# mLSTM gate projection, row-maximum broadcast and denominators in other forms, and the SBUF pools in another order

## The chip, the cores and the metric

One NeuronCore of one Trainium2 chip runs the whole program in one launch. The metric is device time in microseconds of that core, the median of several runs. The kernel before takes 2479.89 us (three runs, 2475.71 to 2484.41). TensorE is the matrix engine, VectorE (DVE), ScalarE (ACT) and GpSimd (POOL) work on tiles of 128 partitions, and SyncE (SP) issues the loads.

## What is computed

Two transformer blocks follow each other on 256 tokens of width 2048, all in float32. The first is attention and a gated feed-forward layer. The second, where the change stands, is an mLSTM beside a gated convolution. Cut to what matters:

```python
proj = h @ w_in[l] + b_in[l]
(q, k, v, o, z_a, i_pre, f_pre, u, b_gate, c_gate, z_b, g_a, g_b) = jnp.split(proj, split_points, axis=-1)
...
b = jnp.cumsum(lf, axis=-1)                       # lf = log_sigmoid(f_pre)
d_intra = b[..., :, None] - b[..., None, :] + li[..., None, :]
m_row = jnp.maximum(d_inter, jnp.max(d_intra, axis=-1))
scores = jnp.einsum('bhld,bhsd->bhls', qb, kb) * jnp.exp(d_intra - m_row[..., None])
num = jnp.einsum('bhls,bhsv->bhlv', scores, vb) + ...
den = jnp.sum(scores, axis=-1) + ...
h_out = num / jnp.maximum(jnp.abs(den), jnp.exp(-m_row))[..., None]
```

There are 8 heads with keys of 128 and values of 256. `i_pre` and `f_pre` are 8 columns each: the projection of the gates is 2048 to 16, beside others of 2048 to 2048.

## The kernel before, in words

A large product is made in fp32r, a fast form of float32, three times over: each operand is split into a high part (`hi`, `khi`) and the rest (`lo`, `klo`), and hi*hi, lo*hi and hi*lo are added in PSUM (`group_mm`, L321 to L323). The work is a list of steps. A step loads a block of weights of 128x2048 (1 MB) into one of four tiles `raw`, splits it (ScalarE makes `hi`, L245, VectorE `lo`, L246) and does 24 matmuls of 512 columns. Loads and splits run ahead of the matmuls by the number of buffers. `later(n, f)` puts a small piece of work behind the matmuls of the step n further on. A scheduler orders the instructions of each engine from this program, by priorities and its own estimate of times; each engine then runs its list in that order.

The second block starts behind a barrier (`barrier2`: norm of the residual, transposes, splits). Then come the steps for v (4 groups of 4 steps), the gates (one step), and four times q/k, o and z_a, with two heads behind each z_a. The rest of the block (`ga`, `u`, `cg`, `bg`, `zb`, `gb`, projections) has no part in the change.

- The gates (`if_step`): weights padded to 128 columns, loaded and split as any step; 3 x 16 x 2 matmuls with 128 moving columns (L983 to L985). `if_rows` turns the result, on 8 partitions, into cumulated rows, their running maximum M and four small transposes (`rowT`).
- A head (`mlstm`) has four pieces. `s1` makes the scores, and a copy of row h of M on all 128 partitions (`mb`, L1082: weights are one column of the identity, repeated, over the 8 partitions of M, in plain float32). `s2` sums the weighted scores over the keys: against a column of ones for the denominators (`den`, L1100 to L1102, three float32 products with one moving column), against the values for the numerators (`num`, L1103 to L1105, three of 256 columns). Six loads of the same three weight tiles belong to them.
- `row_bcast` (L350) copies a gain over all partitions, with a 128x128 tile of ones as weights.
- `pe_gemv` (L194), an adaptive row, is not changed. It is 16 float32 products with 128 moving columns, whose outputs lie on four strips of 32 partitions in turn. The prediction uses its times.

The tiles live in pools which lie one behind the other in SBUF in the order in which the program opens them: single tiles (`persist`), `kp` (40 tiles of 2048 bytes a partition), `zp`, `tp`, `wp` (raw), `hp` (hi, lo), `sp` (small).

## Time and profile before

| what | before |
|---|---|
| median of three runs | 2479.89 us (2475.71 to 2484.41) |
| the profiled execution | 2476.79 us, span 2475.0 us, granted TensorE clock 0.991 |
| TensorE busy | 2410.0 us (97%), 12508 matmul records |
| VectorE busy | 1584.8 us (64%) |
| ScalarE busy | 1151.2 us (47%) |
| DMA | 597.36 MB, 241 GB/s |

The span is the time from the first to the last instruction in the profile; the execution around it is 1.8 us longer. Busy shares are means over the span. A matmul row of the trace gives start, life and count; a float32 product stands there as two records. The granted clock is TensorE's: 1.00 is 2.4 GHz, 0.50 is 1.2 GHz.

### The profile page before, as it was taken

To read this page: it belongs to the slowest core of one execution; us is meant where nothing else is said; L and a number is where in the kernel's file an instruction comes from. 1 tells how busy PE (TensorE), PEld (TensorE's weight loads), DVE (VectorE), ACT (ScalarE), POOL (GpSimd) and SP (SyncE) were. 2 spreads that over 40 slices of the span, in tenths; PEclk is the share of its full clock that TensorE was granted. 3 is DMA by queue.
4 is the path that set the end of the run, shared out by engine and by line. 5 is a ranking of instruction groups with operands and counts; after the bars stand their busy time and mean duration, and the time that the engine had idled before them with its cause. 6 is when DMAs were issued, how large, how long until landed. Compare 5 with 4: busy or idle time off the path is not lost.

```text
span 2475.0 us, 30384 instructions
## 1 busy us (share of the span) xinstructions
PE 2410.0 (97%) x12508; PEld 2023.7 (82%) x12508; DVE 1584.8 (64%) x1727; ACT 1151.2 (47%) x1415; POOL 0.2 (0%) x4
## 2 busy tenths in 40 slices
PE   6999989999999999999899999999999999999998
PEld 4888988878888888888778888888888888888887
DVE  5888888876666566666664556565456666554555
ACT  5433887653443433334553335455333443444344
POOL 0000000000000000000000000000000000000000
PEclk9999999999999999999999999999999999999999
DMA  8987879847777677677635554555557667555553
GB/s 319 339 332 276 312 280 356 335 187 278 287 266 283 252 282 290 240 298 285 217 115 205 184 191 177 188 178 191 187 211 250 242 249 251 201 198 209 189 193 132
DMA packets 90436, 597.36 MB, mean 241 GB/s; under 512 B 10165, under 2 KB 10805, under 8 KB 20665
## 3 DMA queue, kind: packets, MB, share of 16 engines
q1 hardware_dynamic: 90296, 595.41, 66.1%
q8 instruction: 98, 1.61, 0.3%
q14 instruction: 42, 0.34, 0.0%
HBM read 593.28 MB, written 2.10 MB: 241 GB/s over the span
## 4 chain that ended last, share of the span: by engine, by line
PE 89%; DVE 4%; ACT 3%; DMA 3%; issue 1%; SPq 0%; ACTq 0%; DVEq 0%
PE gu L322 6%; PE gu L321 6%; PE gu L323 6%; PE dn L322 3%; PE dn L323 3%; PE dn L321 3%; PE wo L322 2%; PE wo L321 2%; PE wo L323 2%; PE v L321 2%; PE v L322 2%; PE v L323 2%; DVE lo L246 2%; DMA graw<-i_ada_k 2%; PE z_a L321 1%; PE ga L321 1%
## 5 line engine op out<-in xcount | busy, mean ns | idle before, releaser
L246 DVE TENSOR_TENSOR lo<-raw,hi 128x2048 fp32r<-128x2048 f32 (+3 forms) x446 | 917.1, 2061 | 715.2 <-ACT hi L245 714.9
L245 ACT ACTIVATE hi<-raw 128x2048 fp32r<-128x2048 f32 (+3 forms) x446 | 769.1, 1730 | 1037.2 <-PE gu L323 251.3
L321 PE MATMUL gu<-hi,khi 128*128 128x512 f32 x688 | 268.3, 390 | 0.0
L322 PE MATMUL gu<-lo,khi 128*128 128x512 f32 x688 | 267.8, 389 | 0.0
L323 PE MATMUL gu<-hi,klo 128*128 128x512 f32 x688 | 267.7, 389 | 0.0
L172 DVE SCALAR_TENSOR_TENSOR graw<-graw,cb 128x2048 f32<-128x2048 f32 x112 | 255.9, 2285 | 11.1 <-DMA graw<-i_w_ada 8.7
L322 PEld LDWEIGHTS gu<-lo,khi 128*128 128x128 f32 x688 | 129.2, 188 | 26.8 <-DVE lo L246 0.2
L323 PEld LDWEIGHTS gu<-hi,klo 128*128 128x128 f32 x688 | 129.2, 188 | 26.7
L321 PEld LDWEIGHTS gu<-hi,khi 128*128 128x128 f32 x688 | 129.1, 188 | 26.5
L322 PE MATMUL dn<-lo,khi 128*128 128x512 f32 x336 | 131.0, 390 | 1.5 <-DVE lo L246 1.5
L323 PE MATMUL dn<-hi,klo 128*128 128x512 f32 x336 | 130.8, 389 | 0.0
L321 PE MATMUL dn<-hi,khi 128*128 128x512 f32 x336 | 130.5, 390 | 0.0
L285 PE MATMUL qk<-h,lo 128*128 128x256 f32 x256 | 74.7, 292 | 3.1 <-DVE lo L246 3.1
L283 PE MATMUL qk<-h,hi 128*128 128x256 f32 x256 | 75.7, 296 | 0.1
L322 PEld LDWEIGHTS dn<-lo,khi 128*128 128x128 f32 x336 | 63.1, 188 | 15.2 <-DVE lo L246 2.4
L284 PE MATMUL qk<-h,hi 128*128 128x256 f32 x256 | 74.3, 290 | 0.0
L509 PE MATMUL e<-h,lo 128*128 128x256 f32 x256 | 72.8, 287 | 1.6 <-DVE lo L246 1.6
L323 PEld LDWEIGHTS dn<-hi,klo 128*128 128x128 f32 x336 | 63.1, 188 | 13.2
L321 PEld LDWEIGHTS dn<-hi,khi 128*128 128x128 f32 x336 | 63.1, 188 | 13.1
L507 PE MATMUL e<-h,hi 128*128 128x256 f32 x256 | 73.7, 289 | 0.0
L508 PE MATMUL e<-h,hi 128*128 128x256 f32 x256 | 72.9, 286 | 0.0
L285 PEld LDWEIGHTS qk<-h,lo 128*128 128x128 f32 x256 | 51.0, 199 | 3.5 <-DVE lo L246 3.5
(439 smaller groups left out, 4987.1 us busy)
## 6 DMA issues: line engine op xcount, KB each, us to landing
raw<-i_w_gu SPq DMA_DIRECT2D x88, 1024.0 KB, 4.8
graw<-i_ada_t SPq DMA_DIRECT2D x64, 1024.0 KB, 5.9
graw<-i_w_ada SPq DMA_DIRECT2D x48, 1024.0 KB, 4.8
raw<-i_w_dn SPq DMA_DIRECT2D x44, 1024.0 KB, 4.8
graw<-i_ada_k SPq DMA_DIRECT2D x32, 1024.0 KB, 7.0
raw<-i_w_out SPq DMA_DIRECT2D x32, 1024.0 KB, 5.7
raw<-i_w_s SPq DMA_DIRECT2D x24, 1024.0 KB, 6.8
raw<-i_w_qk SPq DMA_DIRECT2D x16, 1024.0 KB, 7.3
```

The lines of the kernel that those rows point to most:

```text
L172: dve.scalar_tensor_tensor(g, g, 1.0, cb, op0=OP.mult, op1=OP.mult, accum_out=dst)
L245: act.activation(hi[:, b:e], r[:, b:e], AF.Copy)
L246: dve.tensor_sub(lo[:, b:e], r[:, b:e], hi[:, b:e].bitcast(F32))
L283: pe.matmul(dst, wh, K[k][:, 0, :], start=s, stop=False)
L284: pe.matmul(dst, wh, K[k][:, 1, :], start=False, stop=False)
L285: pe.matmul(dst, wl, K[k][:, 0, :], start=False, stop=e)
L321: pe.matmul(dsts[th], xh, wh, start=s, stop=False)
L322: pe.matmul(dsts[th], xh, wl, start=False, stop=False)
L323: pe.matmul(dsts[th], xl, wh, start=False, stop=e)
L507: pe.matmul(dst, hv[:, i, c0:c0 + 128], H[k][:, 0, :], start=(k == k0), stop=False)
L508: pe.matmul(dst, hv[:, i, c0:c0 + 128], H[k][:, 1, :], start=False, stop=False)
L509: pe.matmul(dst, lv[:, i, c0:c0 + 128], H[k][:, 0, :], start=False, stop=(k == k1 - 1))
```

## The change

Five edits go together.

- The gates' weights are loaded as they are (128x256, 128 KB), without a step of their own: loaded behind the third group of v, multiplied behind the fourth. The products are plain float32 with 16 weight columns; the inputs are the hi and the lo part one after the other. Block k writes to the strip of partitions 32 (k mod 4); ScalarE copies the four strips into a zeroed tile `ifp`, and two steps later one float32 product with a 0/1 matrix (`mlc["sel"]`) adds them up (`ifq`).
- M is split into hi and lo on partitions 0 to 7 and 32 to 39 of a 64-partition tile (`mhl`), and `mb` is one fp32r product with a repeated column of a 0/1 matrix (`msel`).
- A value tile gets a column of ones behind each 256 values (2 x 260 columns, 2080 bytes), and the denominators come out as column 256 of `num`. There are two output tiles, and ScalarE reads the two columns singly.
- `row_bcast` takes one column of ones, repeated, as weights.
- `zp` is opened behind `hp`; value tiles move into it, `siluz` into `kp`; `epsc` is 208 columns wide and the mask `mM` shares a `z` tile, so that `kp`, `tp`, `wp` and `hp` begin at multiples of 2048 bytes instead of 128 bytes behind such a multiple (the sizes of the tiles give both).

```diff
 K_SEL = 773
-NCONST = 774
+K_MSEL = 774
+K_IF = 782
+NCONST = 846
 def _consts():
...
     c[::32, K_SEL] = 1.0
+    for h in range(8):
+        c[[h, 32 + h], K_MSEL + h] = 1.0
+    for p in range(128):
+        i = p % 16
+        c[p, K_IF + (i if i < 8 else 24 + i)] = 1.0
     return c
...
     kp = ctx.enter_context(tc.tile_pool(name="kp", bufs=40))
-    zp = ctx.enter_context(tc.tile_pool(name="zp", bufs=9))
     tp = ctx.enter_context(tc.tile_pool(name="tp", bufs=TBUFS))
...
     hp = ctx.enter_context(tc.tile_pool(name="hp", bufs=2))
+    zp = ctx.enter_context(tc.tile_pool(name="zp", bufs=9))
     sp = ctx.enter_context(tc.tile_pool(name="sp", bufs=4))
...
     ones = pp.tile([128, 2], F32, name="ones")
-    ksm = pp.tile([128, NCONST - K_INVA], F32, name="ksm")
-    epsc = pp.tile([128, 2], F32, name="epsc")
+    ksm = pp.tile([128, K_IF - K_INVA], F32, name="ksm")
+    epsc = pp.tile([128, 208], F32, name="epsc")
     x = pp.tile([128, 2, D], F32, name="x")
...
         dve.reciprocal(dst, dst)
-    onesr = pp.tile([128, 128], F32R, name="onesr")
-    act.activation(onesr, ones[:, 0:1].to_broadcast([128, 128]), AF.Copy)
+    oner = pp.tile([128, 2], F32R, name="oner")
+    act.activation(oner, ones, AF.Copy)
     def row_bcast(c16, g, grow, key):
...
             for a in range(2):
-                pe.matmul(p, onesr, d[a], start=(a == 0), stop=(a == 1))
+                pe.matmul(p, oner[:, 0:1].to_broadcast([128, 128]), d[a], start=(a == 0), stop=(a == 1))
             if grow is None:
...
     nc.sync.dma_start(ident, A["consts"][:, K_ID:K_ID + 128])
-    nc.sync.dma_start(ksm, A["consts"][:, K_INVA:NCONST])
+    nc.sync.dma_start(ksm, A["consts"][:, K_INVA:K_IF])
     nc.sync.dma_start(x[:, 0, :], A["x"][:, 0, :])
...
     H3 = {}
-    mM = pp.tile([128, 128], F32, name="mM")
     def barrier2():
         assert len(gq) <= 16, len(gq)
-        nc.sync.dma_start(mM, A["consts"][:, K_MM:K_MM + 128])
+        t = ztile("mlc")
+        mlc["hl"] = rtile("mhl")[0:64, 0:S]
+        mlc["M"], mlc["sel"] = t[:, S:S + 128], t[:, S + 128:S + 192]
+        nc.sync.dma_start(mlc["M"], A["consts"][:, K_MM:K_MM + 128])
+        nc.sync.dma_start(mlc["sel"], A["consts"][:, K_IF:K_IF + 64])
+        act.activation(msel, ksm[0:64, K_MSEL - K_INVA:K_MSEL - K_INVA + 8], AF.Copy)
         barrier(H3)
...
-        V2[g, th] = ktile32("v2")
-        dve.tensor_add(V2[g, th], p, b)
-
-    for g in range(4):
-        tok_steps("v", g, v2_evac)
+        t = zp.tile([128, 2, 260], F32, name="v2", tag="z")
+        dve.memset(t[:, :, 256:257], 1.0)
+        dve.tensor_add(t[:, :, 0:256], p.rearrange("p (a c) -> p a c", a=2), b.rearrange("p (a c) -> p a c", a=2))
+        V2[g, th] = t
...
+    msel = pp.tile([64, 8], F32R, name="msel")
+    mlc = {}
...
-    def if_step(hi, lo):
+    def if_load():
+        R["wif"] = ktile32("wif")[:, 0:256]
+        nc.sync.dma_start(R["wif"], A["w_if"])
+
+    def if_post():
+
+        wt = R["wif"]
...
-            dst = p[:, th * 128:(th + 1) * 128]
-            for k in range(KT):
-                wh, wl = hi[:, 128 * k:128 * k + 128], lo[:, 128 * k:128 * k + 128]
-                xh, xl = xs_hl(H3, k, 0, th), xs_hl(H3, k, 1, th)
-                pe.matmul(dst, wh, xh, start=(k == 0), stop=False)
-                pe.matmul(dst, wh, xl, start=False, stop=False)
-                pe.matmul(dst, wl, xh, start=False, stop=(k == KT - 1))
-        if_rows(p)
+            for i in range(4):
+                for a in range(2):
+                    for j in range(4):
+                        k = 4 * i + j
+                        pe.matmul(p[32 * j:32 * j + 16, th * 128:(th + 1) * 128], wt[:, 16 * k:16 * k + 16],
+                                  xs_hl(H3, k, a, th).bitcast(F32), start=(i == 0 and a == 0),
+                                  stop=(i == 3 and a == 1))
+        parts = ttile("ifp")[:, 0:S]
+        dve.memset(parts, 0.0)
+        for j in range(4):
+            act.activation(parts[32 * j:32 * j + 16, :], p[32 * j:32 * j + 16, 0:S], AF.Copy)
+
+        def end():
+            q = acc_tile("ifq")
+            pe.matmul(q[0:64, 0:S], mlc["sel"], parts, start=True, stop=True)
+            if_rows(q)
+        later(2, end)
...
         g = ttile("ifs")[:, :S]
-        act.activation(g, p[:, :S], AF.Identity, bias=cols[:, C_IF:C_IF + 1])
+        act.activation(g[0:64, :], p[0:64, :S], AF.Identity, bias=cols[0:64, C_IF:C_IF + 1])
         f = g[32:40, :]
...
         dve.tensor_sub(u, g[0:8, :], b)
-        M = ztile("rowM")
+        M = ttile("rowM")
         dve.tensor_tensor_scan(M[0:8, 0:S], u, u, 0.0, op0=OP.max, op1=OP.bypass)
...
             dve.tensor_copy(uc, pt[:, 0:32])
-        R["M"] = M
         later(3, tr)
-
-    step(A["w_if"], 2048, if_step)
+        hl = mlc["hl"]
+        act.activation(hl, ones[0:64, 0:1].to_broadcast([64, S]), AF.Copy, scale=0.0)
+        act.activation(hl[0:8, :], M[0:8, 0:S], AF.Copy)
+        dve.tensor_sub(hl[32:40, :], M[0:8, 0:S], hl[0:8, :].bitcast(F32))
+
+
+    for g in range(4):
+        tok_steps("v", g, v2_evac, post=(None, None, if_load, if_post)[g])
     OS = {}
...
         dve.tensor_add(z, p, b)
-        SZ[g, th] = ztile("siluz")
+        SZ[g, th] = ktile32("siluz")
         act.activation(SZ[g, th], z, AF.Tanh, scale=0.5)
...
                 dve.tensor_scalar(hnh, col("headnorm_w_2", 0, 16), 0.5, None, op0=OP.mult)
-            M = R["M"]
             sc = at_tile("st")
...
             mb = at_tile("mb")
-            pe.matmul(mb[:, 0:S], ident[0:8, h:h + 1].to_broadcast([8, 128]), M[0:8, 0:S], start=True,
-                      stop=True)
+            pe.matmul(mb[:, 0:S], msel[:, h:h + 1].to_broadcast([64, 128]), mlc["hl"], start=True, stop=True)
             w = ttile("w")[:, 0:384]
-            dve.scalar_tensor_tensor(w[:, 0:128], mb[:, 0:128], uc[:, h:h + 1], mM, op0=OP.subtract, op1=OP.max)
+            dve.scalar_tensor_tensor(w[:, 0:128], mb[:, 0:128], uc[:, h:h + 1], mlc["M"], op0=OP.subtract, op1=OP.max)
             dve.tensor_scalar(w[:, 128:256], mb[:, 128:256], uc[:, h:h + 1], 0.0, op0=OP.subtract, op1=OP.max)
-            dve.scalar_tensor_tensor(w[:, 256:384], mb[:, 128:256], uc[:, 8 + h:9 + h], mM,
+            dve.scalar_tensor_tensor(w[:, 256:384], mb[:, 128:256], uc[:, 8 + h:9 + h], mlc["M"],
                                      op0=OP.subtract, op1=OP.max)
...
             g, c0 = h // 2, (h % 2) * 256
-            v0 = V2[g, 0][:, c0:c0 + 256]
-            v1 = V2[g, 1][:, c0:c0 + 256]
-            num = at_tile("num")
-            dn = at_tile("den")
-            pe.matmul(dn[:, 0:1], w[:, 0:128], ones[:, 0:1], start=True, stop=True)
-            pe.matmul(dn[:, 1:2], w[:, 128:256], ones[:, 0:1], start=True, stop=False)
-            pe.matmul(dn[:, 1:2], w[:, 256:384], ones[:, 0:1], start=False, stop=True)
-            pe.matmul(num[:, 0:256], w[:, 0:128], v0, start=True, stop=True)
-            pe.matmul(num[:, 256:512], w[:, 128:256], v0, start=True, stop=False)
-            pe.matmul(num[:, 256:512], w[:, 256:384], v1, start=False, stop=True)
+            v0 = V2[g, 0][:, h % 2, 0:257]
+            v1 = V2[g, 1][:, h % 2, 0:257]
+            num = [at_tile("num") for _ in range(2)]
+            pe.matmul(num[0][:, 0:257], w[:, 0:128], v0, start=True, stop=True)
+            pe.matmul(num[1][:, 0:257], w[:, 128:256], v0, start=True, stop=False)
+            pe.matmul(num[1][:, 0:257], w[:, 256:384], v1, start=False, stop=True)
             da = small("da")
-            act.activation(da[:, 0:2], dn[:, 0:2], AF.Abs)
+            for i in range(2):
+                act.activation(da[:, i:i + 1], num[i][:, 256:257], AF.Abs)
             ss = small("mss")
...
             for i in range(2):
-                dve.scalar_tensor_tensor(t[:, i * 256:(i + 1) * 256], num[:, i * 256:(i + 1) * 256],
+                dve.scalar_tensor_tensor(t[:, i * 256:(i + 1) * 256], num[i][:, 0:256],
                                          da[:, i:i + 1], OS[g, i][:, c0:c0 + 256], op0=OP.mult, op1=OP.mult)
...
         a["w_" + name + "2"] = _groups(w[:, o:o + n])
-    wif = np.zeros((D, 128), np.float32)
-    wif[:, 0:8] = w[:, 8192:8200]
-    wif[:, 32:40] = w[:, 8200:8208]
-    a["w_if"] = _blocks(wif)[0]
+    a["w_if"] = np.ascontiguousarray(w[:, 8192:8208].reshape(KT, 128, 16).transpose(1, 0, 2)).reshape(128, 256)
     a["w_pa"] = _groups(g["w_proj_a_2"][0])
```

The scheduler's lists for TensorE, at the three places that the prediction speaks of. First the gate projection, between the last group of v and the first of q. Before, the last rows of v and the first of the projection's 96:

```order
L321 MATMUL v_10769<-hi,khi 128x512
L322 MATMUL v_10769<-lo,khi 128x512
L323 MATMUL v_10769<-hi,klo 128x512
L983 MATMUL if<-khi,hi 128x128
L984 MATMUL if<-klo,hi 128x128
L985 MATMUL if<-khi,lo 128x128
```

Of the change, the end of the projection (it has 16 such rows, 64 products) with q behind it:

```order
L1001 MATMUL if<-khi,wif 16x128 x4
L1001 MATMUL if<-klo,wif 16x128 x4
L328 MATMUL q_10981<-hi,khi 128x512
L329 MATMUL q_10981<-lo,khi 128x512
L330 MATMUL q_10981<-hi,klo 128x512
```

The place is the same, the 96 matmuls are 64 products on 16 output partitions. The product that adds the strips stands some 50 rows further on, between two steps of q:

```order
L329 MATMUL q_10982<-lo,khi 128x512
L330 MATMUL q_10982<-hi,klo 128x512
L1011 MATMUL ifq<-ifp,mlc 64x256
L328 MATMUL q_10981<-hi,khi 128x512
L329 MATMUL q_10981<-lo,khi 128x512
```

Second, the first head's scores and broadcast (`st`, `mb`) with the transposes of the next head (`qkT`) behind them. Before:

```order
L1079 MATMUL st<-mqk 128x256
L1080 MATMUL st<-mqk 128x128
L1082 MATMUL mb<-rowM,ident 128x256
L1069 MATMUL qkT<-ident,tq 128x128 x2
L1069 MATMUL qkT<-ident,tk 128x128 x2
```

Of the change:

```order
L1110 MATMUL st<-mqk 128x256
L1111 MATMUL st<-mqk 128x128
L1113 MATMUL mb<-mhl,msel 128x256
L1101 MATMUL qkT<-ident,tq 128x128 x2
L1101 MATMUL qkT<-ident,tk 128x128 x2
```

Nothing moved; the operands of `mb` are others. Third, the first head's denominators and numerators, with a step of o around them. Before:

```order
L323 MATMUL o_11555<-hi,klo 128x512
L1100 MATMUL den<-ones,w 128x1
L1101 MATMUL den<-ones,w 128x1
L1102 MATMUL den<-ones,w 128x1
L1103 MATMUL num<-v_10502,w 128x256
L1104 MATMUL num<-v_10502,w 128x256
L1105 MATMUL num<-v_10504,w 128x256
L321 MATMUL o_11554<-hi,khi 128x512
```

Of the change:

```order
L330 MATMUL o_11542<-hi,klo 128x512
L1129 MATMUL num<-v_10506,w 128x257
L1130 MATMUL num<-v_10506,w 128x257
L1131 MATMUL num<-v_10509,w 128x257
L328 MATMUL o_11541<-hi,khi 128x512
```

The three products with one column are gone, and the numerators have one column more.

## Rows read from the trace of the kernel before

**Rows 1.** The page: busy time of each engine, and TensorE's clock in 40 slices.

```profile
PE 2410.0 (97%) x12508; PEld 2023.7 (82%) x12508; DVE 1584.8 (64%) x1727; ACT 1151.2 (47%) x1415; POOL 0.2 (0%) x4
PEclk9999999999999999999999999999999999999999
```

**Rows 2.** Waits of TensorE from 1245 us on: total, times, longest in us.

```profile
PE v L321 <- ACT khi L297: 2.7, 2, 1.4
PE rowT L1024 <- DVE rowB L1015: 0.5, 1, 0.5
```

**Rows 3.** Two stretches (v, heads): length, engines busy (x instructions), clock, DMA share, GB/s.

```profile
1297.00:1360.00 63.00, 63.00 (x279) 52.10 (x278) 30.96 (x21) 21.63 (x14) 0.00 (x0) 1.00 0.58 202
1500.00:1700.00 200.00, 200.00 (x924) 165.01 (x923) 117.69 (x148) 102.29 (x114) 0.00 (x0) 1.00 0.50 178
```

**Rows 4.** TensorE timeline, both ends of the gate projection: start, life in us.

```profile
1360.94 0.22 PE L983 MATMUL if<-khi,hi 128*128 128x128 f32 x1
...
1371.61 0.45 PE L321 MATMUL q<-hi,khi 128*128 128x512 f32 x1
1371.90 0.40 PE L322 MATMUL q<-lo,khi 128*128 128x512 f32 x1
```

**Rows 5.** Timeline of TensorE, one adaptive row between large matmuls.

```profile
145.46 0.39 PE L323 MATMUL v<-hi,h 128*128 128x512 f32 x1
145.78 1.08 PE L194 MATMUL gv<-graw,cols 128*32 128x128 f32 x32
146.79 0.50 PE L321 MATMUL v<-hi,h 128*128 128x512 f32 x1
147.13 0.40 PE L322 MATMUL v<-lo,h 128*128 128x512 f32 x1
```

**Rows 6.** Timeline of TensorE, first head, piece s1.

```profile
1471.62 0.59 PE L1079 MATMUL st<-mqk 128*128 128x256 f32 x2
1472.05 0.38 PE L1080 MATMUL st<-mqk 128*128 128x128 f32 x2
1472.36 0.69 PE L1082 MATMUL mb<-rowM,ident 8*128 8x256 f32 x2
1472.99 0.44 PE L1069 MATMUL qkT<-ident,tq 128*128 128x128 f32 x2
```

**Rows 7.** Timeline of TensorE, first head, piece s2.

```profile
1478.94 0.28 PE L1100 MATMUL den<-ones,w 128*128 128x1 f32 x2
...
1479.52 0.68 PE L1103 MATMUL num<-v,w 128*128 128x256 f32 x2
1480.04 0.59 PE L1104 MATMUL num<-v,w 128*128 128x256 f32 x2
1480.47 0.59 PE L1105 MATMUL num<-v,w 128*128 128x256 f32 x2
1480.71 0.59 PE L321 MATMUL o<-hi,khi 128*128 128x512 f32 x1
1481.14 0.40 PE L322 MATMUL o<-lo,khi 128*128 128x512 f32 x1
```

**Rows 8.** Tile gu: shortest, median and longest life in ns, first and last start.

```profile
L321 PEld LDWEIGHTS gu<-hi,khi x688: 187/188/192, 513.1 to 1137.8; 128*128 128x128 f32 x172
L321 PE MATMUL gu<-hi,khi x688: 389/389/478, 513.3 to 1138.0; 128*128 128x512 f32 x172
```

**Rows 9.** Timeline of TensorE, matmuls of 256 columns; L508 reads the other half.

```profile
213.56 0.28 PE L507 MATMUL e<-h,hi 128*128 128x256 f32 x1
213.69 0.28 PE L508 MATMUL e<-h,hi 128*128 128x256 f32 x1
213.81 0.28 PE L509 MATMUL e<-h,lo 128*128 128x256 f32 x1
```

**Rows 10.** Timelines: VectorE, a small fill; ScalarE, line of the denominators.

```profile
0.83 0.06 DVE L166 MEMSET epsc<- 128x1 f32 x1
...
1481.00 0.15 ACT L1107 ACTIVATE da<-den 128x2 f32<-128x2 f32 x1
```

## The prediction

> **What bounds the kernel now.** I read the page first, for the share of each engine [rows 1]: TensorE is busy for 97% of the span, VectorE for 64%, ScalarE for 47%, and the clock digits of TensorE are nines. One number over the span says little about one stage, so next come two stretches where the changed work stands, the v steps behind the second barrier and the first heads [rows 3]: TensorE is busy without a gap, at a granted clock of 1.00 (its upper level, 2.4 GHz), while VectorE has about two fifths of each stretch free and the DMA engines close to half. Then the waits, to see whether anything in these stretches holds TensorE up [rows 2]: after 1245 us the two that matter are 2.7 us at the barrier and 0.5 us at the small transposes of the gate rows. So here a microsecond taken off TensorE's queue is a microsecond off the end, and work taken off the other engines is worth nothing by itself. Of 63.00 us there, 279 large matmuls take 0.226 each, a step of 24 thus 5.4 us in which VectorE and ScalarE split the next block.
>
> How to read a matmul row: the second column is its life from first to last, and lives overlap. What it costs the queue is the distance from its start to the start of the next.
>
> **The gate projection.** Before, it takes 96 matmuls of 128 columns, from 1360.94 to 1371.61 us, 10.67 us, and the large matmul behind it stands 0.29 from its successor instead of 0.23, so 10.73 [rows 4]. They stand 0.11 us apart although 128 columns at 2.4 GHz are 0.053 us: each pays for its own 128x128 weight load. Now there are 64 products in plain float32, 16 weight columns wide, put on four strips of output partitions in turn. Float32 products are two passes in this trace (32 records for the 16 products of one adaptive row), so 128 passes. The nearest row is that adaptive row: also float32, 128 moving columns, four strips in turn, 32 passes [rows 5]. From the start of the large matmul ahead of it (145.46) to the start of the second one behind it (147.13) are 1.67 us; less two large ones, 1.21. Inside, 32 passes of eight groups are 1.01 us to the next start, of which some 0.14 is the last gap, so 0.87 goes by groups (0.109 each) and 0.34 by entering and leaving. The projection has 32 groups in one visit: 4 x 0.87 + 0.34 = 3.8 us. Bounds: 4 x 0.87 = 3.5, and four full visits, 4 x 1.21 = 4.8. Gain 6.9 us (5.9 to 7.2).
>
> The four strips have to be added up: one float32 product of 256 columns, two steps later. The pair of such passes at 1471.62 takes 0.43 us [rows 6]; its output is 64 wide, so it may pay for entering and leaving too. I take 0.55 (0.43 to 0.77). What hangs on it (four small ScalarE copies, the row arithmetic, 78 matmul rows later the transposes) has about 17 us of TensorE work as cover, as it had 73 rows before, with a wait of 0.5 [rows 2]; up to 1 us more if the order is unlucky.
>
> The step that goes also had a load of 1 MB and a split; a load of 128 KB comes in its place. In the built program SP's bias loads move a few places forward past large loads, and wait for matmuls of the block before the barrier, which are long done when SP comes to them. Cost nothing, covered by the free DMA half [rows 3].
>
> **The broadcast of the row maximum** (once for each of eight heads). Before: L1080 starts at 1472.05 and is two passes of 128 columns, so 0.22; the broadcast starts at 1472.36, 0.09 late, and the transposes at 1472.99, 0.63 behind it [rows 6]. Its two passes are thus about 0.1 us dearer each than a 256-column pass with all 128 rows. Now it is one fp32r pass over 64 rows. A fp32r pass of 256 columns stands 0.12 us from the next where all rows are used [rows 9]; half of what the old form takes, 0.31, is the other end, since the new one also uses part of the rows. I take 0.22: nearer the first because one pass is left, with one change of form. Gain 0.41 each, 3.3 us in all (2.5 to 4.1).
>
> **The denominators.** Before, six passes with one moving column [rows 7]: 1478.94 to 1479.52 are 0.58 us, about 0.11 for each pass after the first, as long as the weights take to load; and the first pass of the numerators stands 0.52 from the third instead of 0.43 for two passes. Now the ones are the 257th column of the values, and the same six weight loads lie under passes of 0.216. Three products are 6 x 0.216 less 0.19 (the last row's distance is 0.24 for two, and the rest falls to the next large matmul, as before) = 1.11 us, against 1.77 from 1478.94 to 1480.71. Gain 0.66 each, 5.3 us in all; lower bound 8 x 0.58 = 4.6. The extra column is 2 clocks a pass, 48 passes, 0.04 us.
>
> Here a rule of the Trainium skill speaks against the size of the gain: "TensorE: Matmul & The Clock Gate", section "Wait — 56ns, not 53.3ns?", says that starts of very small matmuls come down to about 25 ns. By that the 48 passes would be only an estimated 1.2 us, and the sum below would be smaller by some 4 us. The trace does not agree where each pass has weights of its own: the passes stand 0.11 us apart [rows 7], and the sum goes by that.
>
> **What else moves.** ScalarE reads each denominator column by itself, 8 more instructions of 0.15 us [rows 10], with 3 us of slack behind them. VectorE gets eight fills of two elements (0.06 us each [rows 10]) between the barrier's additions, where it waits for ScalarE anyway, and one of 256 columns: 0 to 0.7 us on the barrier's path. The 24 row broadcasts take their weights from one column repeated instead of from 128; the adaptive rows already do that without a visible price [rows 5], so 0, and as the dear bound 24 x 0.09 = 2.2 us, the extra of the old broadcast. Up to the second barrier the order on every engine is the same but for one 64x8 copy on ScalarE, which falls into the start, before x has landed, and two small loads of constants on SP.
>
> **The addresses.** By the sizes of the tiles, all pools that feed TensorE start 128 bytes past a multiple of 2048 before, and at one after. Does that matter to the 10,464 large fp32r matmuls? Weight slices of 512 bytes then begin at 128, 640, 1152 and 1664; the last runs over the 2048 line. All 688 loads of one line take 187 to 192 ns and its matmuls have one median [rows 8], so crossing costs nothing; nor do the two halves of the moving operand differ, one of which crosses [rows 9]. I take 0.
>
> **Sum.** -6.9 + 0.55 - 3.3 - 5.3 = -15.0 us. Cheapest case: -7.2 + 0.4 - 4.1 - 5.4 = -16.3. Dearest: -5.9 + 0.8 - 2.5 - 4.6 + 2.2 + 0.7 + 1 = -8.3. The profiled execution took 2476.8 us; the median of the runs is 3.1 more, 2479.9. So 2461.8 by the former, and **2465** for a median. With both ends and the runs' own spread (4.2 below, 4.5 above the median) the forecast alone reaches from 2459 to 2476.
>
> **Rivals.**
> 1. *The strips do not overlap.* With other weights for each product the four strips might run one behind the other. Then 128 passes at the old 0.11 us are 14.1 instead of 3.8, the sum falls to -4.7, and the time is 2475. For it: changes of form do cost 0.1 us here [rows 6]. Against: the adaptive rows also change weights with each product [rows 5]. A clock that falls in or behind these sparse 4 us would go the same way, by a few us. Chance 0.09.
> 2. *The address does matter, for the better.* A large fp32r matmul stands 227 ns from the next; 512 columns at 2.4 GHz are 213, and a 256-column one has the same 13 ns over [rows 9]. A float32 pass of 256 columns, at two clocks a column, has 3 over (216 against 213 [rows 7]). If the offset of 128 bytes, 32 columns of four bytes, were what costs the 13, all would drop: up to 10,464 x 0.010 = 105 us, to 2360. Against: no offset in this trace shows a difference, though all share the 128 bytes. Chance 0.07. The Trainium skill ("TensorE: Matmul & The Clock Gate", "Back-to-back issue gap") gives columns / 2.4 + 2.5 ns, an estimated 216 for 512: the trace does not reach it in fp32r.
> 3. *It matters for the worse*, which makes the kernel slower. The gain is eaten up when each large matmul costs 15.0 / 10,464 = 1.4 ns more, for instance because tiles of one engine now begin on the same line as the reads of another. With 3 ns, of the 5 between the shortest and the longest weight load [rows 8], it is +31 - 15, or 2496. Against: the same as for the second. Chance 0.05.
>
> **Chances.** Forecast 0.79, rivals 0.09, 0.07, 0.05. A measurement of this kernel can tell about 0.3%, 7.4 us. The forecast gives faster in nearly all of its cases (its dearest end gives no change), the first rival gives no change, the second faster, the third slower: faster 0.83, same 0.12, slower 0.05. The range takes the forecast's own ends, the first rival at the top, and 3 us at the bottom for a small part of the second (0.3 ns a matmul): 2456 to 2476.
>
> **What would show it.** Right: between the last value matmul and the first q matmul some 3.8 us; broadcasts of 0.2 to 0.3 us to the transposes behind; no denominator matmuls and 1.1 us for the numerators; 12,486 TensorE records (128 + 2 more, 96 + 48 + 8 fewer); the large matmuls still 0.227 us apart. Wrong: groups of the projection further apart than 0.11 us, a new wait of TensorE for the gate rows or at the barrier, a clock below 1.00 behind the projection, or another distance of the large matmuls anywhere in the span.

## The result, and the profile after

The changed kernel takes **2462.7 us** (median of 4 runs, 2459.1 to 2466.1), the kernel before 2479.7 (4 runs, 2475.7 to 2484.4): a ratio of 0.9933, 95% interval 0.9921 to 0.9945, or 17.0 us less (13.6 to 19.6). The forecast was 2465, in a range of 2456 to 2476. The profiled execution took 2464.4 us.

The page of the profile after, busy time of each engine and TensorE's clock (to be read beside [rows 1]):

```profile
PE 2395.4 (97%) x12486; PEld 2009.0 (82%) x12486; DVE 1583.0 (64%) x1736; ACT 1151.5 (47%) x1429; POOL 0.2 (0%) x4
PEclk9999999999999999999999999999999999999999
```

The waits of TensorE from 1245 us on (total, times, longest; [rows 2]), and the same two stretches as in [rows 3]:

```profile
PE v L328 <- ACT khi L304: 2.7, 2, 1.4
...
PE rowT L1051 <- DVE rowB L1042: 0.2, 1, 0.2
```

```profile
1297.00:1360.00 63.00, 63.00 (x279) 51.80 (x278) 30.73 (x23) 23.84 (x17) 0.00 (x0) 1.00 0.60 216
```

```profile
1500.00:1700.00 200.00, 200.00 (x909) 165.30 (x908) 122.59 (x154) 103.55 (x119) 0.00 (x0) 1.00 0.52 186
```

TensorE is still what bounds the time: 14.6 us of its busy time are gone, and the other engines are as they were. The waits are the old ones, and the stretch of v holds the same 279 matmuls in 63 us. The wait at the row transposes did not grow (0.2 us, 0.5 before), and the clock stayed at 1.00.

Where the time went is read from the timeline of TensorE after. The gate projection's first rows ([rows 4] before), the product that adds the strips, and q around it:

```profile
1362.70 0.39 PE L330 MATMUL v<-hi,klo 128*128 128x512 f32 x1
1363.02 0.41 PE L1001 MATMUL if<-khi,wif 128*16 128x128 f32 x8
1363.25 0.40 PE L1001 MATMUL if<-klo,wif 128*16 128x128 f32 x8
1363.47 0.40 PE L1001 MATMUL if<-khi,wif 128*16 128x128 f32 x8
...
1366.64 0.50 PE L328 MATMUL q<-hi,khi 128*128 128x512 f32 x1
...
1377.42 0.39 PE L330 MATMUL q<-hi,klo 128*128 128x512 f32 x1
1377.74 0.65 PE L1011 MATMUL ifq<-ifp,mlc 128*64 128x256 f32 x2
1378.32 0.50 PE L328 MATMUL q<-hi,khi 128*128 128x512 f32 x1
1378.66 0.39 PE L329 MATMUL q<-lo,khi 128*128 128x512 f32 x1
```

The first head's scores and broadcast ([rows 6] before), and its numerators ([rows 7] before):

```profile
1467.15 0.59 PE L1110 MATMUL st<-mqk 128*128 128x256 f32 x2
1467.58 0.38 PE L1111 MATMUL st<-mqk 128*128 128x128 f32 x2
1467.89 0.38 PE L1113 MATMUL mb<-mhl,msel 64*128 64x256 f32 x1
1468.20 0.44 PE L1101 MATMUL qkT<-ident,tq 128*128 128x128 f32 x2
```

```profile
1474.19 0.59 PE L1129 MATMUL num<-v,w 128*128 128x257 f32 x2
1474.62 0.60 PE L1130 MATMUL num<-v,w 128*128 128x257 f32 x2
1475.05 0.60 PE L1131 MATMUL num<-v,w 128*128 128x257 f32 x2
1475.30 0.58 PE L328 MATMUL o<-hi,khi 128*128 128x512 f32 x1
```

Eight passes of the projection take 0.22 us (1363.25 to 1363.47), so four go in 0.11, and the whole takes 3.62 (1363.02 to 1366.64). The broadcast stands 0.31 ahead of the transposes (0.63 before). The numerators start right behind o and need 1.11 us.

Summed over the trace, from the start of one pass to the start of the next and with what the neighbouring passes lose or gain: gate projection -6.91 (10.67 become 3.62; neighbours +0.14), strip-adding product +0.78, broadcasts -2.50 (4.99 become 2.49), denominators -5.33 (4.68 for themselves, 0.65 in the first numerator). That is -14.0. Between the two profiled executions the start-up gives back some 2 us (waits for the first DMAs, which differ from run to run); the medians differ by 3 us more than the sum, which is still inside the interval of 13.6 to 19.6.

### The profile page after: what moved, and what is told of

Its sections match the earlier page's. It is cut to its first block, busy times and chain, and to the rows that moved or that the text cites. A ratio compares the mean times of both kernels' runs of the same rounds, so it can differ in the third digit from the quotient of the medians.

```text
span 2462.3 us, 30366 instructions
## 1 busy us (share of the span) xinstructions
PE 2395.4 (97%) x12486; PEld 2009.0 (82%) x12486; DVE 1583.0 (64%) x1736; ACT 1151.5 (47%) x1429; POOL 0.2 (0%) x4
## 4 chain that ended last, share of the span: by engine, by line
PE 90%; ACT 4%; DVE 3%; DMA 2%; issue 1%; SPq 0%; ACTq 0%; DVEq 0%
PE gu L328 6%; PE gu L329 6%; PE gu L330 6%; PE dn L329 3%; PE dn L330 3%; PE dn L328 3%; PE wo L329 2%; PE wo L328 2%; PE wo L330 2%; PE v L328 2%; PE v L329 2%; PE v L330 2%; DVE lo L253 2%; PE z_a L328 1%; PE ga L328 1%; PE o L330 1%
## 5 line engine op out<-in xcount | busy, mean ns | idle before, releaser
L328 PE MATMUL v<-hi,h 128*128 128x512 f32 x128 | 51.6, 411 | 2.5 <-ACT hi L252 2.5
```

The costliest lines, as they stand in the source:

```text
L328: pe.matmul(dsts[th], xh, wh, start=s, stop=False)
```

## Experiments

All times stand against 2462.7 us of the changed kernel; each ratio is to the kernel before, measured beside the run on the same chip. Beside these runs the kernel before took 2479.1 to 2480.7 us, so a difference of a microsecond or two between times is not a result by itself, and the traces decide there. A *visit* is below a run of neighbouring passes of one form, other than that of the passes around it.

### One part undone at a time

**den_apart**: the three one-column products return.

```diff
-            num = [at_tile("num") for _ in range(2)]
-            pe.matmul(num[0][:, 0:257], w[:, 0:128], v0, start=True, stop=True)
...
+            dn = at_tile("den")
+            pe.matmul(dn[:, 0:1], w[:, 0:128], ones[:, 0:1], start=True, stop=True)
+            pe.matmul(dn[:, 1:2], w[:, 128:256], ones[:, 0:1], start=True, stop=False)
+            pe.matmul(dn[:, 1:2], w[:, 256:384], ones[:, 0:1], start=False, stop=True)
...
```

> The changed kernel with the denominators as three float32 products with one moving column again, ahead of the numerators; all else as changed. Theory: the six weight loads of a head have no passes to lie under, and a head pays 0.58 us for the denominators and 0.08 us more on the first numerator; 8 x 0.66 = 5.3 us of the gain go, so 2462.7 + 5.3 = 2468 (ratio to the kernel before 0.9955). In the trace the den passes stand 0.11 us apart, and the first pass of num stands 0.30 from the second. Rival (starts of very small matmuls come down to 25 ns): 48 passes cost about 1.2 us, so 2464. Rival (the heads were hidden behind other work and the gain came from elsewhere): 2463.

Measured: 2469.4 us, ratio 0.9957 (0.9945 to 0.9970), 6.7 more. The timeline of its first head:

```profile
1474.56 0.28 PE L1131 MATMUL den<-ones,w 128*128 128x1 f32 x2
1474.70 0.36 PE L1132 MATMUL den<-ones,w 128*128 128x1 f32 x2
1474.92 0.36 PE L1133 MATMUL den<-ones,w 128*128 128x1 f32 x2
1475.14 0.68 PE L1134 MATMUL num<-v,w 128*128 128x256 f32 x2
```

From 1474.56 to 1475.14 are 0.58 us for six passes, and the first numerator pass stands 0.299 from the second instead of 0.216. Both terms of the 5.3 us are back in the trace; the rival with 25 ns a pass falls.

**mb_old**: the broadcast in float32 over 8 rows.

```diff
-        mlc["hl"] = rtile("mhl")[0:64, 0:S]
+        mlc["hl"] = ktile32("mhl")[0:8, 0:S]
...
-            pe.matmul(mb[:, 0:S], msel[:, h:h + 1].to_broadcast([64, 128]), mlc["hl"], start=True, stop=True)
+            pe.matmul(mb[:, 0:S], ident[0:8, h:h + 1].to_broadcast([8, 128]), mlc["hl"], start=True, stop=True)
```

> The changed kernel with the broadcast of the row maximum as a float32 product over 8 rows again; all else as changed. The trace after shows 0.311 us from the start of the fp32r broadcast to the start behind it. Theory: the old form costs 0.62 us each again, so 8 x 0.31 = 2.5 us of the gain go: 2465.2 (0.994). The prediction's 0.41 each would be 3.3 us: 2466. Rival (a price per change of tile form, not per pass): the difference is one pass of 0.22 at the most, 8 x 0.22 = 1.8 us: 2464.5. The trace decides between them by the distance of mb to the transposes; the times alone can't.

Measured: 2466.8 us, 0.9945 (0.9931 to 0.9958). The interval overlaps that of the changed kernel, so the trace decides. Its first head:

```profile
1466.74 0.69 PE L1111 MATMUL mb<-mhl,ident 8*128 8x256 f32 x2
1467.37 0.44 PE L1099 MATMUL qkT<-ident,tq 128*128 128x128 f32 x2
```

All eight broadcasts together take 4.99 us instead of 2.49, two passes of 0.319 and 0.305 each. By the trace this part is worth 2.5 us.

**if_old**: the projection as a step of 96 products with 128x128 weights.

```diff
-        tok_steps("v", g, v2_evac, post=(None, None, if_load, if_post)[g])
+        tok_steps("v", g, v2_evac)
+
+    step(A["w_if"], 2048, if_step)
...
```

> The changed kernel with the gate projection as a step of its own again: 96 fp32r matmuls of 128 columns with 128x128 weights, a load of 1 MB and a split; no strips and no adding product. Theory: 10.67 us in place of 3.62 + 0.58, so +6.5 us: 2469 (0.9958), and the passes stand 0.11 apart. Rival (the load of 1 MB and the split, 2048 columns on VectorE and ScalarE, were part of the price): more than 6.5, up to 8, with a stall of TensorE ahead of the step. Rival (the time came from the order of the steps around it): less than 4 us.

Measured: 2469.2 us, 0.9953 (0.9941 to 0.9966), 6.5 more. Both ends of the projection:

```profile
1361.77 0.39 PE L330 MATMUL v<-hi,klo 128*128 128x512 f32 x1
1361.99 0.22 PE L995 MATMUL if<-khi,hi 128*128 128x128 f32 x1
...
1372.55 0.28 PE L997 MATMUL if<-khi,lo 128*128 128x128 f32 x1
1372.66 0.45 PE L328 MATMUL q<-hi,khi 128*128 128x512 f32 x1
```

The passes stand 0.11 apart, the projection takes 10.67 us (1361.99 to 1372.66), and TensorE does not wait ahead of it. So the 1 MB load and the split were free, as forecast.

The three undone parts give 6.7 + 4.1 + 6.5 = 17.3 us by the times and some 14 by the ratios, beside 17.0 measured and 14.0 in the trace of the change: no other part is needed to explain it. The row broadcasts were not undone singly; in the trace most of their passes stand 235 ns from the next instead of 231, which is 0.1 us for all 24.

### Do the four strips run beside each other?

**strips_apart** changes the order of the loops alone:

```diff
-            for i in range(4):
-                for a in range(2):
-                    for j in range(4):
+            for j in range(4):
+                for i in range(4):
+                    for a in range(2):
```

> The changed kernel with the 64 products of the gate projection ordered strip by strip: the sixteen of one strip of output partitions, then the next strip, for each half of the tokens; the sums are the same. Theory: products on four strips in turn run beside each other, four in the 0.109 us of two clocks a column at 128 columns; on one strip they can't, so 128 passes at 0.109 us are 14 us instead of 3.6, +10.3 us: 2473. Rival (the strips don't run beside each other, the passes are cheap because their weights are 16 columns wide): no change, 2462.7.

Measured: 2472.2 us, 0.9972 (0.9959 to 0.9984), 9.5 more. Its timeline:

```profile
1362.10 0.39 PE L1001 MATMUL if<-khi,wif 128*16 128x128 f32 x2
1362.33 0.38 PE L1001 MATMUL if<-klo,wif 128*16 128x128 f32 x2
1362.55 0.38 PE L1001 MATMUL if<-khi,wif 128*16 128x128 f32 x2
```

Two passes now take 0.22 us where eight did. Start to start the passes are 0.109 apart on one strip. Only at the seven changes of strip do starts close up, four times each (0.005 to 0.018), so that the visit is 11.13 us instead of the 14 that I expected; in the changed kernel it is 3.62. By the trace the cost is thus 7.5 us; the 9.5 of the times agree with that within their intervals. Narrow weights alone gain nothing, the turn over the strips does.

### What the broadcast pays for

**mb_128** and **mb_f128** use all 128 rows, the added ones zero, the first in fp32r, the second in float32 (the edit of mb_128; mb_f128 takes the column of the identity as mb_old does):

```diff
-        mlc["hl"] = rtile("mhl")[0:64, 0:S]
+        mlc["hl"] = rtile("mhl")[:, 0:S]
...
-            pe.matmul(mb[:, 0:S], msel[:, h:h + 1].to_broadcast([64, 128]), mlc["hl"], start=True, stop=True)
+            pe.matmul(mb[:, 0:S], msel[:, h:h + 1].to_broadcast([128, 128]), mlc["hl"], start=True, stop=True)
```

> The changed kernel with the fp32r broadcast of the row maximum over all 128 rows (the rows that are added hold zeros) instead of 64. Theory: 0.31 us is the price of a pass that uses part of the rows, whatever its type, since the float32 passes over 8 rows also stand 0.31 apart; with all rows an fp32r pass of 256 columns goes in 0.12 us, and the transposes behind start without a delay: 8 x 0.19 = 1.5 us less, about 2461 (0.9927), and up to 8 x 0.3 = 2.4 if the passes beside it gain too. Rival (the change between float32 and fp32r costs, not the rows): mb stays at 0.25 or more, no gain.

> The broadcast of the row maximum in float32 over all 128 rows (zeros in 120 of them), no split into two parts; all else as changed. Theory (a price for part of the rows): two passes 0.216 us apart, 0.43 in all, so 8 x 0.12 = 1 us more than the changed kernel: 2463.7. Rival (the price is that of a change of type): no change of type in this order, two passes of 0.216 as well, but then the fp32r form over 128 rows stays at 0.31; the two runs together decide. Rival (the weights' single repeated column is the price): the passes stay 0.31 apart.

Measured: 2460.6 us, 0.9930 (0.9916 to 0.9943), and 2463.7, 0.9942 (0.9930 to 0.9955). The first heads of mb_128 and of mb_f128:

```profile
1467.77 0.38 PE L1111 MATMUL st<-mqk 128*128 128x128 f32 x2
1467.91 0.37 PE L1113 MATMUL mb<-mhl,msel 128*128 128x256 f32 x1
1468.11 0.38 PE L1101 MATMUL qkT<-ident,tq 128*128 128x128 f32 x2
```

```profile
1468.41 0.60 PE L1111 MATMUL mb<-mhl,ident 128*128 128x256 f32 x2
1468.85 0.38 PE L1099 MATMUL qkT<-ident,tq 128*128 128x128 f32 x2
```

In mb_128, from the last pass of `st` to the transposes are 0.234 us (0.031 and 0.203), what a 128-column float32 pass and a 256-column fp32r pass take anywhere (0.109 + 0.120). In the changed kernel the same piece is 0.516 (0.204 and 0.312), and the pass behind the first transpose starts 0.058 late: 0.345 us are paid for using 64 rows. The type costs nothing, since the fp32r pass beside float32 ones has no price left, and the float32 form over all rows is 0.218 and 0.216. My expectation that each *pass* with part of the rows costs 0.31 was wrong. The price is paid once per visit: the old form took 0.624 + 0.205 + 0.058, 0.887 in all, where its three passes are 0.541 without a price (0.109 + 2 x 0.216); the new one took 0.574 where 0.229 would do. Both differences are 0.345. In the four heads with a large matmul behind the broadcast instead of transposes the price is 0.39, and 0.40 in the old form.

By the traces mb_128 is some 2.9 us better than the change (0.34 in four heads, 0.39 in the other four). The medians (2460.6, 2462.7) point the same way but their intervals overlap, so a gain in time is likely, not shown.

### The addresses

**pools_1248** moves all pools that feed TensorE together, **zp_front** only undoes the move of the pool with the value tiles, which are 2080 bytes wide and so displace what lies behind them by 9 x 32 = 288 bytes:

```diff
-    epsc = pp.tile([128, 208], F32, name="epsc")
+    epsc = pp.tile([128, 2], F32, name="epsc")
```

> The changed kernel with a two-column constant in place of the one of 208, so that all pools that feed TensorE start 1248 bytes past a multiple of 2048. Theory: the address is without effect; 2462.7 within 3 us, and the large fp32r matmuls of 512 columns stand 227.0 ns apart, those of 256 columns 119.8. Rival (the address sets the pace): another distance; each nanosecond is 10.5 us over 10,464 matmuls.

```diff
     kp = ctx.enter_context(tc.tile_pool(name="kp", bufs=40))
+    zp = ctx.enter_context(tc.tile_pool(name="zp", bufs=9))
     tp = ctx.enter_context(tc.tile_pool(name="tp", bufs=TBUFS))
...
-    zp = ctx.enter_context(tc.tile_pool(name="zp", bufs=9))
```

> The changed kernel with the pool of the wider value tiles back ahead of the pools of raw weights and of split weights, which moves those off multiples of 2048 bytes by its own odd size; all else as changed. Theory: without effect, 2462.7 within 3 us, large passes 227.0 ns apart. Rival (weight tiles that begin off a multiple of 2048 load more slowly): another distance, each nanosecond 10.5 us.

Measured: pools_1248 2462.4 us, 0.9935 (0.9922 to 0.9948): no effect. **zp_front 2515.0 us, 1.0147 (1.0133 to 1.0160)**: 52.4 slower than the changed kernel and 35 slower than the one before. I had expected no effect. Its order of instructions on TensorE is the same, and its waits differ by less than 2 us in all; the lines with most matmuls and a full stretch, first of the kernel after, then of zp_front:

```profile
L328 PE MATMUL gu<-hi,khi 128*128 128x512 f32 x688 | 268.3, 390 | 0.0
```

```profile
2000.00:2100.00 100.00, 100.00 (x451) 82.76 (x450) 65.00 (x59) 41.11 (x34) 0.00 (x0) 1.00 0.69 243
```

```profile
L328 PE MATMUL gu<-hi,khi 128*128 128x512 f32 x688 | 272.7, 397 | 0.0
```

```profile
2000.00:2100.00 100.00, 100.00 (x443) 80.80 (x442) 64.50 (x55) 40.51 (x33) 0.00 (x0) 1.00 0.71 252
```

TensorE is busy without a gap at clock 1.00 in both, but each matmul lives 7 ns longer and 443 instead of 451 fit. Which addresses do it? **offsets** puts 32 bytes behind each token tile (38 of them instead of 40, so that they fit) and 288 behind each buffer of split weights, so that many distances occur in one run:

```diff
-        return kp.tile([128, 512], F32R, name=name, tag="k")
+        return kp.tile([128, 520], F32R, name=name, tag="k")[:, 0:512]
...
-            hi = hp.tile([128, 2048], F32R, name="hi", tag="hi")
+            hi = hp.tile([128, 2120], F32R, name="hi", tag="hi")[:, 0:2048]
...
```

> The changed kernel with 32 bytes of padding behind each 2048-byte tile of the pool with the token operands (38 buffers in place of 40, so that it fits) and 288 bytes behind each buffer of split weights, which thus start at 1216, 1504, 1792 and 32 past a multiple of 2048: the products meet their two operands at all distances in steps of 32 bytes. The run before showed 233.2 ns for a 512-column pass with the moving operand 288 bytes past the stationary one (modulo 512) and 227.0 with both on the same offset, and 118.3 against 119.8 for 256 columns. Theory A (the distance of the two operands' addresses sets the pace): sorted by that distance the passes fall into sharp groups, 227 at a distance of 0 modulo 512 or a divisor of it, 233 elsewhere, and so the kernel takes some 2500 us. Theory B (the moving operand's own address sets the pace): sorted by the four starts of the split weights they fall into sharp groups, and the distance makes no difference within one. Theory C (the stationary operand's own address): groups by the forty starts of the token tiles. Theory D (not the addresses of TensorE's operands but those that VectorE and ScalarE read and write): no groups by either, the same pace everywhere, near 227.

Measured: 2507.7 us (one run). The 227 of theory D did not come, and none of the others got its sharp groups. Nearly all 512-column passes stand 224 to 239 ns apart, 232.1 on average. By the four starts of the split weights the means are 231.3 to 232.4. The 180 passes whose two operands, and the next weights, agree modulo 512 also have 232.1. Passes that repeat the same three addresses agree better (spread 1.8 ns, against 3.3 over all), so addresses matter, but not by a rule for single passes. Two orders of the pools then decide between the engines, and a third run tries another distance (the order of the pools in each, in words; kp holds the token tiles, hp the split weights, wp the raw ones, tp small tiles, zp the value tiles):

```text
kp, tp, wp, hp, zp   (the changed kernel)
kp, tp, wp, zp, hp   (hp_last: split weights displaced)
kp, hp, zp, tp, wp   (hp_first: tp and the raw weights displaced)
kp, zp, tp, wp, hp   (zp_front_2112: value tiles of 264 columns instead of 260)
```

> The changed kernel with one pool moved: that of the split weights (hi and lo) behind the pool of the wider value tiles, so that it alone starts 288 bytes past a multiple of 2048; the raw weights that VectorE and ScalarE read stay where the changed kernel has them. Theory A (the two operands of TensorE must start on the same offset modulo 512, in the whole stretch and not in single passes): as with the value tiles ahead of all three pools, 233 ns a 512-column pass and 2515 us. Theory D (the raw weights against the split ones, that is VectorE and ScalarE, take TensorE's turn at the memory): raw and split are now 288 apart where they were together before, so something else than 233 or 227.

> The changed kernel with the pool of split weights directly behind that of the token operands (both at multiples of 2048), then the value tiles, then small tiles and raw weights, which start 288 bytes past a multiple of 2048. Theory A: TensorE's two operands stand together, so 227 ns and 2462.7 us within 3. Theory D: the operands of VectorE and ScalarE are now as far apart as in the slow kernel's products, so 230 or more and over 2490 us.

> The changed kernel with the value tiles ahead again but 264 columns wide (2112 bytes instead of 2080), which moves the three pools behind them by 576 bytes, 64 modulo 512, where the slow kernel had 288. Theory A with a short period (a distance that is a multiple of 64 is as good as none): 227 ns and 2463 us. Theory A with the period of 512: 230 ns or more, over 2490 us.

Measured: hp_last 2516.2 us, 1.0147 (1.0129 to 1.0165); hp_first 2465.0, 0.9940 (0.9925 to 0.9955); zp_front_2112 2478.0, 0.9994 (0.9984 to 1.0003). The page's line of gu in the three, in that order:

```profile
L328 PE MATMUL gu<-hi,khi 128*128 128x512 f32 x688 | 272.4, 396 | 0.0
```

```profile
L328 PE MATMUL gu<-hi,khi 128*128 128x512 f32 x688 | 268.3, 390 | 0.0
```

```profile
L328 PE MATMUL gu<-hi,khi 128*128 128x512 f32 x688 | 271.1, 394 | 0.0
```

So it is the pair of TensorE's own operands, token tiles against split weights; where the raw weights of VectorE and ScalarE stand does not matter. The mean distances from start to start of the fp32r passes (without those over 245 and 132 ns, which hold a wait or a change of form; the starts, in bytes past a multiple of 2048, follow from the sizes of the tiles):

| split weights against token tiles | kernels | 512 columns, ns | 256 columns, ns |
|---|---|---|---|
| 0, both at 128 | before | 227.0 | 119.8 |
| 0, both at 0 | after, hp_first | 227.0 | 119.8 |
| 0, both at 1248 | pools_1248 | 227.0 | 119.8 |
| 64 (576) | zp_front_2112 | 229.1 | 114.3 |
| 288 | zp_front, hp_last | 233.2 | 118.3 |

With 512 columns the split weights move and the token tiles are loaded, with 256 it is the other way round. With 8,928 passes of 512 columns and 1,536 of 256, 8,928 x 6.2 less 1,536 x 1.5 ns is 53 us, the 52.4 measured. At 64, 8,928 x 2.1 less 1,536 x 5.5 is 10; measured are 15, of which 2.6 more stand in DMA waits at the start and the rest is not explained.

The slow kernels hold a test of their own. A few steps keep their split weights in kp (`khi`, `klo` on both sides of a product), so that both operands share an offset there while those of the steps around them do not. Such a step of zp_front, 24 passes, and the first pass behind it:

```profile
1270.08 0.40 PE L328 MATMUL dn<-khi 128*128 128x512 f32 x1
...
1272.16 0.39 PE L328 MATMUL dn<-khi 128*128 128x512 f32 x1
...
1275.56 0.40 PE L328 MATMUL dn<-hi,khi 128*128 128x512 f32 x1
```

The first nine passes stand 230.7 ns apart, the fifteen behind them 226.7. In hp_last it is 230.8 and 226.7, in the changed kernel 226.7 for all 24. So the pair decides within one run too, but a pace is reached only some nine passes after the last pass of the other kind. In offsets the distance changes with nearly every pass, which may be why agreeing passes do not get to 227 there; that was not tested.

Not tried: other distances, and 64 for the 256-column products alone, which by the table would be 1,536 x 5.5 = 8 us better than the change. The period of the effect and the mechanism behind it stay open.

## Why the prediction was right, and where it was not

- **What bounds.** Right: every microsecond taken off TensorE behind the second barrier came off the end. The three parts undone singly add up to the whole, within the spread of the runs.
- **Gate projection**, -6.9: -6.91 in the trace. The row it rested on [rows 5], with 0.109 a group and 0.34 for entering and leaving, carried over: 0.109 and 0.33. The first rival falls: strips do run beside each other, and in strips_apart, where nearly all neighbours share a strip, the projection takes 11.1 us. That is less than the 14.1 which the rival counted.
- **Strip-adding product**, +0.55: +0.78, just past the upper bound (0.77). Its two passes take 0.43 as always; entering, leaving and the late successor are another 0.35, not the 0.12 that I allowed.
- **Broadcast**, -3.3: -2.5, the dear end. The failed step is "about 0.1 us dearer each", a price per pass read from [rows 6]. The price is per visit, so the change took off only passes (2 x 0.216 less 0.120 is 0.312, 8 x 0.312 = 2.5) and left 0.34 to 0.39 a head standing. The prediction had 0.34 for entering and leaving the adaptive row, and did not use it here. mb_128 showed it.
- **Denominators**, -5.3: -5.33. The floor from the Trainium skill that was weighed there ("TensorE: Matmul & The Clock Gate", "Wait — 56ns, not 53.3ns?", 25 ns for very small matmuls) is not what binds these passes: den_apart has 0.58 us for six again.
- **Everything else**, 0: right. The 1 MB load and the split were covered, the rows' wait shrank to 0.2 us, the barrier's waits are 2.7 as before, and the row broadcasts cost 0.1 us of the 2.2 allowed.
- **Addresses**, 0: right for the change as made, by a reason that is too wide. "I take 0" rested on the fact that no offset in the trace made a difference; but in that trace both operands of the large products always shared one offset, and the change moved both together, from 128 to 0. Had the wider value tiles stayed ahead of the split weights, a step that the prediction did not price at all, the kernel would have been 35 us slower than before. The third rival (3 ns a matmul for the worse) named the direction and half the size: 6.2 ns, in a case that the change avoids. The prediction gave the distance between the two operands no price, so the 0 is partly luck.
- **The sum** was -15.0; the trace has -14.0, the medians -17.0. Both misses (0.8 and 0.2 us) lie at the dear ends of their terms. The median came out 2 us below the forecast although the trace's sum is 1 us short of it: that nearness lies within the spread of the runs and is luck, not mechanism.

## What to carry to other kernels

Price a small product by its visit: here 0.33 to 0.40 us for each change to fewer rows or columns and back, whatever number of passes lies between, and next to nothing for a change of type; so fill the rows with zeros, or make many passes in one visit. Where weights are narrow, the gain comes from going round the strips of output partitions with neighbouring products, not from the narrowness. And before a tile gets a few columns more, look at which pools lie behind it: the large products here ran fastest with both operands on one common offset, and each of their 512-column passes paid 2 to 6 ns when they lost it.

## What the runs showed of the hardware

- The start addresses of TensorE's two operands against each other change its pace: 227.0 ns a 512-column pass at a distance of 0, 229.1 at 64 and 233.2 at 288 bytes; a common shift (0, 128, 1248) does nothing. Where the distance goes back to 0 in the middle of a slow run, 227 is reached after nine passes (zp_front, hp_last). The Trainium skill ("TensorE: Matmul & The Clock Gate", "Step-by-step: what each phase is for") says that the moving operand and the weight load have ports of their own, and that loading the next weights takes no bandwidth from the running matmul. No run here shows whether that holds: the same instructions in the same order differ by 6 ns a pass with the addresses alone, but whether the weight load is what gets in the way was not shown.
- For 256-column passes with the roles exchanged, 64 bytes are better than 0 (114.3 against 119.8 ns).
- A visit with fewer rows (8 or 64 of 128) or fewer output columns (16, 64) costs 0.33 to 0.40 us over its passes in all four places: projection (0.33), strip-adding product (0.345), old and new broadcast (0.345 with transposes behind, 0.39 to 0.40 with a large matmul behind). Of it, 0.09 falls to the pass ahead (0.318 instead of 0.227) and up to 0.11 to the one behind (0.338). The Trainium skill ("TensorEngine Tiling (Array Packing)", "Key Properties") says that a change of the tiling mode drains TensorE, and gives no figure; the runs agree that the change is what costs, with 0.33 to 0.40 us for there and back.
